# The outer dimension of a broadcast load and of a scattered store in a triangular inverse

## The chip, the cores and the metric

The kernel runs on one core of a Trainium2 chip. The metric is the device time of one execution in microseconds (us). Three runs of the kernel before took 3386.37, 3397.44 and 3398.57 us; their median is 3397.44 us.

## What is computed

A backbone of two layers works on 512 latent tokens and 256 context tokens of width 1024. Each layer has three parallel token mixers (a gated linear attention, a windowed attention, and RWKV-7 time mixing), whose outputs are gated, merged and projected, and then a SwiGLU feed-forward part. The change lies in the third mixer, which the reference runs forward and backward over the tokens, eight heads of 64, one token at a time:

```python
def step(S, inp):
    w_t, k_t, v_t, kk_t, a_t = inp[:5]
    sa = jnp.einsum('bhvk,bhk->bhv', S, kk_t)
    S = S * w_t[:, :, None, :] - sa[..., None] * (kk_t * a_t)[:, :, None, :] + v_t[..., None] * k_t[:, :, None, :]
    return S, jnp.einsum('bhvk,bhk->bhv', S, inp[5])
```

All operands are float32, and every matrix product of the layers is made of three with operands split in two parts (`wh`, `wl` of the weights, `hh`, `hl` of the activations).

## The kernel before

**The recurrence in chunks.** Class `Rwkv` takes the 768 tokens in 24 chunks of 32, four chunks to a group, six groups to each direction. The directions are two lanes, f and b, that `run` advances in turns (`lanes`, `ORDER`). For each group and lane three generators run: `prep` scales the loaded keys (`cp`, `kr`, `bk`, loaded by `load`) and makes the small products `X` on PE, masked by DVE (line 1507); `inverse` makes from `X` the inverse of one 32x32 unit triangular matrix per chunk and head; `chain` carries the state over the four chunks with `TT`, the inverses, as PE's weights (line 1595). `front` is `prep` followed by `inverse`; it runs one group ahead of `chain` in layer 0 and two groups in layer 1 (`ahead`). So there are 12 inverses in each layer, 24 in all.

**The inverse.** Two DMAs (line 1530) write the 32 triangular matrices of a group (4 chunks x 8 heads) from `X` to DRAM as `d1`, one after the other, 4 KB each. One DMA (line 1532) loads them into `L`, a tile of 128 partitions x 1024 floats: matrix m goes to partitions m, 32 + m, 64 + m and 96 + m, all four holding the same 4 KB. Partition 32 s + m then works on every fourth row of matrix m's inverse, the rows 4 a + s. `G` (128 x 8 x 32) starts as the rows of the identity: ACT issues a DMA from the constant `gid` (line 1537, called the reset here). In 31 steps of two instructions (line 1548, product into `ftmp`; line 1549, subtraction from `G`) the substitution is done, on DVE for lane f and on POOL for lane b. One DMA (line 1552) stores `G` to DRAM as `d2`, in runs of 32 floats, and one (line 1554) loads it in the layout that `chain` wants, as `TT`.

**What sets the order.** `L` and `G` have two buffers each, shared by both lanes. So an `L` is issued when the substitution two back has read its last, and a reset when the store two back has landed. Nearly all loads and stores are issued by SP, in one order, and each one can stand there for a semaphore; ACT issues the reset, `uv` and the store of the gates `gs` in its own stream of work. The completion of DMAs is counted on eight semaphores (DMAHW0 to DMAHW7 in the rows of order below), which are taken in turn: a DMA waits for the one that had its semaphore before. A planner (`TileContext` with its own model of times) decides the order of the instructions on each engine at build time, from the order of the generators and the dependences.

**What lies beside it.** In layer 0, `fill` gives PE projections (16 gate jobs and 8 branch jobs) between the lanes' turns. In layer 1 the same jobs are tied to the recurrence by `paced`: past a start of 150 products, 3.3 products are let go for every step noted by `hop`.

Of the kernel before, what the change touches and what calls it, by code (L numbers as in the profile page):

```python
# [1216 lines left out]
class Rwkv:  # L1217
# [304 lines left out]
    def inverse(self, d, g, later):  # L1522

        nc, T = self.nc, self.T
        d1 = self.D.tile([2, 16, 32, 32], F32, name="d1", tag="d1", bufs=3)
        d2 = self.D.tile([8, 4, 32, 32], F32, name="d2", tag="d2", bufs=3)
        X = self.hs[d, g]["X"]
        for q in range(2):
            r0 = 0 if q == 0 else 96
            nc.sync.dma_start(d1[q].rearrange("u j i -> j u i"), X[r0:r0 + 32].rearrange("j e w p i -> j (e w p) i")[:, :, 0:32])  # L1530
        L = T.tile([128, 32, 32], F32, name="L", tag="L", bufs=2)
        nc.sync.dma_start(L.rearrange("u j i -> u (j i)"), d1.rearrange("q u j i -> (q u) (j i)").unsqueeze(0).to_broadcast([4, 32, 1024]))
        yield
        if later is not None:
            self.load(d, later)
        G = T.tile([128, 8, 32], F32, name="G", tag="G", bufs=2)
        nc.scalar.dma_start(G, self.I["gid"])
        tmp = T.tile([128, 128], F32, name="ftmp", tag="ftmp", bufs=2)
        eng = nc.vector if d == "f" else nc.gpsimd
        for n in range(31):  # L1540
            if d == "f":
                j, rows, cols = n, slice(0, n // 4 + 1), slice(n + 1, 32)
            else:
                j = 31 - n
                rows, cols = slice(j // 4, 8), slice(0, j)
            a, m = rows.stop - rows.start, cols.stop - cols.start
            t = tmp[:, 0:a * m].rearrange("q (a b) -> q a b", b=m)
            eng.tensor_tensor(out=t, in0=G[:, rows, j:j + 1].to_broadcast([128, a, m]), in1=L[:, j:j + 1, cols].to_broadcast([128, a, m]), op=ALU.mult)  # L1548
            eng.tensor_tensor(out=G[:, rows, cols], in0=G[:, rows, cols], in1=t, op=ALU.subtract)  # L1549
            if n % 8 == 7:  # L1550
                yield
        nc.sync.dma_start(d2.rearrange("m p (a s) i -> s (m p) a i", s=4), G)
        TT = self.hs[d, g]["TT"] = T.tile([128, 8, 32], F32, name="TT", tag="TT", bufs=4 if self.zout else 6)
        nc.sync.dma_start(TT, d2.rearrange("m p r i -> (p r) m i"))
        yield
# [177 lines left out]
def _consts():  # L1733
    f = np.float32
    C = {}
    p = np.arange(128)
    C["ident"] = np.eye(128, dtype=f)
    o = np.zeros((128, 32), f)
    o[:, 0] = 1
    C["ones32"] = o  # L1740
    sn = np.zeros((128, 4, 128), f)
    for j in range(4):
        sn[32 * j, j, :] = 1
    C["selN"] = sn
    s = np.zeros((128, 4, 32), f)
    for j in range(4):
        s[:64, j, 2 * j] = 1
        s[64:, j, 2 * j + 1] = 1
    C["selH"] = s
    C["selkk"] = np.ascontiguousarray(np.tile(s.transpose(2, 1, 0), (4, 1, 1)))  # L1750
    j, i = (p % 32)[:, None], np.arange(32)[None, :]
    m = np.zeros((128, 2, 64), f)
    m[:, 0, :32], m[:, 0, 32:] = j < i, j <= i
    m[:, 1, :32], m[:, 1, 32:] = j > i, j >= i
    C["rmask"] = m
    g = np.zeros((128, 8, 32), f)
    for s_ in range(4):
        for a in range(8):
            g[32 * s_:32 * s_ + 32, a, 4 * a + s_] = 1
    C["gid"] = g  # L1760

    T = np.arange(512)
    inv = 10000.0 ** (-np.arange(16, dtype=np.float32) / np.float32(16))
    inv = inv.astype(np.float32)
    row, col = (T // 64).astype(f), (T % 64).astype(f)
    ang = np.stack([row[:, None] * inv, col[:, None] * inv], 1).astype(f)
    cs, sn_ = np.cos(ang).astype(f), np.sin(ang).astype(f)
    cos = np.zeros((128, 512), f)
    sin = np.zeros((128, 512), f)
    rot = np.zeros((128, 128), f)  # L1770
    for h in range(2):
        for a in range(2):
            for x in range(2):
                for q in range(16):
                    r = 64 * h + 32 * a + 16 * x + q
                    cos[r], sin[r] = cs[:, a, q], sn_[:, a, q]
                    if x == 0:
                        rot[r + 16, r] = -1.0
                    else:
                        rot[r - 16, r] = 1.0  # L1780
    C["cos"], C["sin"], C["rot"] = cos, sin, rot

    gm = np.zeros((5, 128, 32), np.int32)
    for n, mm in enumerate((16, 8, 4, 2, 1)):
        a, b = (p % 32)[:, None], np.arange(32)[None, :]
        gm[n] = (a // (2 * mm) == b // (2 * mm)) & (a // mm != b // mm)
    C["gmask"] = np.ascontiguousarray(gm.transpose(1, 0, 2))
    C["gdiag"] = (2.0 * ((p % 32)[:, None] == np.arange(32)[None, :])).astype(f)
    sm = np.ones((128, 768), f)
    sm[:, ::128] = 0  # L1790
    C["gscan"] = sm
    import ml_dtypes
    q_, k_ = np.arange(128)[:, None], np.arange(128)[None, :]
    w = np.zeros((128, 2, 128), f)
    w[:, 0] = np.where(k_ >= q_, 0.0, -1e30)
    w[:, 1] = np.where(k_ <= q_, 0.0, -1e30)
    C["wmask"] = w.astype(ml_dtypes.bfloat16)
    C["identb"] = np.eye(128, dtype=f).astype(ml_dtypes.bfloat16)
    return C


def _layout(x, c, ctx, c_ctx, w_ada, b_ada, g_mix, g_ffn, w_in, w_gk2, b_gk, g_gla, sink, mu_shift, w0, w_w2, a0, w_a2,
# [58 lines left out]
    D["w3"] = tile_k(w_ffn3, HID)  # L1861
    D["w2"] = con(w_ffn2.reshape(L, HID, 128, 8, 128).transpose(0, 3, 2, 1, 4)).reshape(L, 8, 128, HID * 128)
    D.update(_consts())
    return D

# [14 lines left out]
```

## Time and profile before

| | before |
|---|---|
| median of three runs | 3397.44 us |
| profiled execution, its own time | 3397.11 us |
| its span | 3394.7 us |
| granted TensorE clock, mean of the span | 0.911 |
| PE busy | 3014.1 us (89%) |
| DVE, ACT, POOL busy | 1725.6, 1126.2, 942.1 us |
| DMA moved | 398.31 MB, mean 117 GB/s |

The profile is one execution. A row of a timeline gives start, duration and, in brackets, how long the engine had been idle and what ended that; a letter q behind an engine's name (SPq, ACTq) means its queue, where a DMA's duration is that of its issue, not of the transfer. In the chain of waits a DMA's piece runs from its issue to its landing. The names d<-X, L<-d, d<-G, TT<-d and G<-gid are the five DMAs of the inverse. PE is TensorE, DVE VectorE, ACT ScalarE, POOL GpSimd, SP SyncE. The granted clock is a share of 2.4 GHz.

### The profile page before, as it was taken

What the parts mean: (1) busy time and instruction counts of PE and PEld (TensorE: products, weight loads), DVE (VectorE), ACT (ScalarE), POOL (GpSimd) and SP (SyncE); (2) the same over time, 40 slices, a digit from 0 to 9 for tenths busy, and PEclk for the clock granted to TensorE, in tenths of its full rate; (3) what the DMA queues carried; (4) which work ended last, traced back from release to release, by engine and by line L of the source; (5) the groups of instructions that cost most, each with busy time, mean ns of one, the idle gap of its engine ahead of it and who ended that gap; (6) DMA issues with size and microseconds to landing.
All of it is one profiled execution on the core that took longest, in us unless ns stands there. A gap on an engine that the chain in (4) does not pass through costs nothing. (4 is left out here: it accounts for less than half of the span.)

```text
span 3394.7 us, 62575 instructions
## 1 busy us (share of the span) xinstructions
PE 3014.1 (89%) x25760; PEld 2403.8 (71%) x25760; DVE 1725.6 (51%) x3336; ACT 1126.2 (33%) x2226; POOL 942.1 (28%) x1344
## 2 busy tenths in 40 slices
PE   6999999867888989999999899698757779799998
PEld 3777877655666778888888787576535456688887
DVE  3175557756546754222223455656556665643335
ACT  3255444422323333211112444543222233332223
POOL 2033122245346432100001212322256454221102
PEclk8999999877787999999999899899867789799999
DMA  7421222543335561443222323123533444613233
GB/s 286 152 73 61 96 101 96 174 118 104 103 110 145 179 203 57 154 155 139 62 69 89 95 75 97 57 77 132 177 99 111 126 122 142 190 58 100 93 100 118
DMA packets 269373, 398.31 MB, mean 117 GB/s; under 512 B 94624, under 2 KB 179360, under 8 KB 269088
## 3 DMA queue, kind: packets, MB, share of 16 engines
q1 hardware_dynamic: 241888, 360.76, 33.7%
q10 hardware_dynamic: 27200, 33.56, 3.0%
q8 instruction: 202, 3.31, 0.4%
q14 instruction: 83, 0.68, 0.1%
HBM read 320.33 MB, written 73.92 MB: 116 GB/s over the span
## 5 line engine op out<-in xcount | busy, mean ns | idle before, releaser
L50 PE MATMUL px<-hh,wh 128*128 128x512 f32 x1584 | 657.1, 415 | 21.8 <-ACT wh L71 15.3
L50 PE MATMUL px<-hh,wl 128*128 128x512 f32 x1584 | 649.2, 410 | 29.4 <-DVE wl L72 29.4
L50 PE MATMUL px<-hl,wh 128*128 128x512 f32 x1584 | 647.2, 409 | 10.4 <-POOL hl L302 7.9
L71 ACT ACTIVATE wh<-raw 128x1024 fp32r<-128x1024 f32 (+1 forms) x314 | 326.2, 1041 | 834.2 <-PE pz L50 411.9
L72 DVE TENSOR_TENSOR wl<-raw,wh 128x1024 fp32r<-128x1024 f32 (+1 forms) x314 | 398.3, 1269 | 369.6 <-ACT wh L71 336.5
L50 PEld LDWEIGHTS px<-hh,wh 128*128 128x128 f32 x1584 | 312.3, 197 | 115.6 <-issue 24.5
L50 PEld LDWEIGHTS px<-hh,wl 128*128 128x128 f32 x1584 | 311.5, 197 | 107.3 <-DVE wl L72 34.6
L50 PEld LDWEIGHTS px<-hl,wh 128*128 128x128 f32 x1584 | 312.3, 197 | 82.9 <-POOL hl L302 13.1
L673 POOL TENSOR_TENSOR al<-fs,ah 128x768 fp32r<-128x768 f32 (+1 forms) x44 | 85.0, 1931 | 728.1 <-ACT ah L672 728.1
L50 PE MATMUL pz<-hh,wh 128*128 128x256 f32 x872 | 254.5, 293 | 1.5 <-DVE fs L663 1.4
L50 PE MATMUL pz<-hl,wh 128*128 128x256 f32 x872 | 253.9, 291 | 2.2 <-DVE hl L304 1.7
L50 PE MATMUL pz<-hh,wl 128*128 128x256 f32 x872 | 253.2, 291 | 1.3 <-DVE wl L72 0.8
L50 PE MATMUL px<-y,wh 128*128 128x512 f32 (+1 forms) x512 | 152.6, 386 | 31.6 <-ACT y L123 14.1
L1548 POOL TENSOR_TENSOR ftmp<-G,L 128x60 f32<-128x60 f32 (+24 forms) x372 | 133.2, 358 | 165.8 <-DMA L<-d 78.7
L50 PEld LDWEIGHTS pz<-hh,wh 128*128 128x128 f32 x872 | 171.8, 198 | 10.1 <-issue 1.8
L50 PEld LDWEIGHTS pz<-hl,wh 128*128 128x128 f32 x872 | 172.5, 198 | 8.2 <-issue 2.2
L50 PEld LDWEIGHTS pz<-hh,wl 128*128 128x128 f32 x872 | 171.9, 197 | 6.4 <-issue 4.6
L1548 DVE TENSOR_TENSOR ftmp<-G,L 128x60 f32<-128x60 f32 (+24 forms) x372 | 106.1, 285 | 96.7 <-DMA L<-d 45.4
L1549 POOL TENSOR_TENSOR G<-G,ftmp 128x60 f32<-128x60 f32 (+24 forms) x372 | 137.0, 368 | 26.6
L50 PEld LDWEIGHTS px<-y,wh 128*128 128x128 f32 x512 | 95.4, 209 | 50.3 <-ACT y L123 14.9
L1603 ACT COPY uv<-up 32x128 f32<-32x128 f32 x384 | 98.2, 256 | 68.0 <-PE up L1595 50.7
L50 PE MATMUL px<-ah,wh 128*128 128x512 f32 x296 | 116.1, 393 | 0.0
(444 smaller groups left out, 5952.9 us busy)
## 6 DMA issues: line engine op xcount, KB each, us to landing
raw<-win SPq DMA_DIRECT2D x114, 512.0 KB
raw<-w SPq DMA_DIRECT2D x104, 512.0 KB
araw<-wada SPq DMA_DIRECT2D x96, 512.0 KB
raw<-w SPq DMA_DIRECT2D x48, 448.0 KB
kr<-krd SPq DMA_DIRECT2D x24, 512.0 KB
L<-d SPq DMA_DIRECT2D x24, 512.0 KB
gs<-gat ACTq DMA_DIRECT2D x24, 384.0 KB
raw<-wab SPq DMA_DIRECT2D x16, 512.0 KB
```

The costliest lines, as they stand in the source:

```text
L50: return self.nc.tensor.matmul(out, lhsT=lhsT, rhs=rhs, start=start, stop=stop)
L71: nc.scalar.activation(h[:, :n], raw[:, :n], AF.Copy)
L72: nc.vector.tensor_tensor(out=lo[:, :n], in0=raw[:, :n], in1=h[:, :n].bitcast(F32), op=ALU.subtract)
L673: nc.gpsimd.tensor_tensor(out=al, in0=s, in1=ah.bitcast(F32), op=ALU.subtract)
L1548: eng.tensor_tensor(out=t, in0=G[:, rows, j:j + 1].to_broadcast([128, a, m]), in1=L[:, j:j + 1, cols].to_broadcast([128, a, m]), op=ALU.mult)
L1549: eng.tensor_tensor(out=G[:, rows, cols], in0=G[:, rows, cols], in1=t, op=ALU.subtract)
L1603: nc.scalar.copy(uv[ru, p].rearrange("q e v -> q (e v)"), up[32 * p:32 * p + 32, :])
```

## The change

```diff
@@ inverse @@
         L = T.tile([128, 32, 32], F32, name="L", tag="L", bufs=2)
-        nc.sync.dma_start(L.rearrange("u j i -> u (j i)"), d1.rearrange("q u j i -> (q u) (j i)").unsqueeze(0).to_broadcast([4, 32, 1024]))
+        nc.sync.dma_start(L.rearrange("u j i -> u (j i)"), d1.rearrange("q u j i -> (q u) (j i)").unsqueeze(1).to_broadcast([32, 4, 1024]))
...
-        nc.sync.dma_start(d2.rearrange("m p (a s) i -> s (m p) a i", s=4), G)
+        for s in range(4):
+            nc.sync.dma_start(d2.rearrange("m p (a s) i -> s (m p) a i", s=4)[s], G[s::4])
@@ _consts @@
     for s_ in range(4):
         for a in range(8):
-            g[32 * s_:32 * s_ + 32, a, 4 * a + s_] = 1
+            g[s_::4, a, 4 * a + s_] = 1
```

Matrix m now goes to partitions 4 m to 4 m + 3, so that the load's source steps through 32 matrices outermost and repeats each four times, where it stepped through 4 copies of all 32. Partition 4 m + s works on the rows 4 a + s; the constant `gid` follows. The store is cut in four, one for each s, each from 32 partitions (every fourth) into 32 blocks of `d2`. The bytes are the same: 512 KB for a load of `L`, 128 KB for the four stores of one `G`. SP issues 72 DMAs more (4 for 1, 24 times). Lines behind 1552 move down by one.

The planner's order changes in the two recurrence stages. On SP, at the second round of layer 1, before (DVE_49 and Pool_49 are waits for lane f's and lane b's substitution):

```order
L1532 DMA L<-d_23411 128x1x1024 [waits DMAHW2_49,DVE_49]
L1552 DMA d_23134<-G 4x256x32 [waits DMAHW3_49,DVE_49]
L1532 DMA L<-d_23417 128x1x1024 [waits DMAHW6_49,DMAHW7_49,DMAHW4_49,Pool_49]
L1552 DMA d_23140<-G 4x256x32 [waits DMAHW5_49,Pool_49]
L1554 DMA TT<-d_23134 128x8x32 [waits DMAHW3_49]
```

and now:

```order
L1532 DMA L<-d_23453 128x1x1024 [waits DMAHW6_49,DVE_49]
L1553 DMA d_23170<-G 256x1x32 [waits DMAHW7_49,DVE_49]
L1553 DMA d_23170<-G 256x1x32 [waits DMAHW0_49]
L1553 DMA d_23170<-G 256x1x32 [waits DMAHW1_49]
L1553 DMA d_23170<-G 256x1x32 [waits DMAHW2_49]
L1553 DMA d_23176<-G 256x1x32 [waits DMAHW3_49,Pool_49]
L1553 DMA d_23176<-G 256x1x32 [waits DMAHW4_49]
L1555 DMA TT<-d_23170 128x8x32 [waits DMAHW6_49,DMAHW2_49,DMAHW7_49,DMAHW1_49,DMAHW0_49]
L1553 DMA d_23176<-G 256x1x32 x2
L1532 DMA L<-d_23459 128x1x1024
```

Lane b's load of `L` stood between the two stores; now it stands behind lane b's stores and behind lane f's `TT`, which waits for lane f's four stores.

On DVE, where the second substitution of lane f in layer 1 begins (X is the mask of lane b's products, on which PE's transposes and `d1` hang), before:

```order
L1480 SCALAR_TENSOR_TENSOR cs<-smask,cp 128x544
L1507 TENSOR_TENSOR X<-xp,rmask 128x512
L1488 COPY pc<-cp 128x16
L1507 TENSOR_TENSOR X<-xp,rmask 128x512
L1512 TENSOR_TENSOR bk<-bk,pc 128x1024
L1548 TENSOR_TENSOR ftmp<-G,L 128x31
L1549 TENSOR_TENSOR G<-G,ftmp 128x31
L1548 TENSOR_TENSOR ftmp<-G,L 128x30
```

and now:

```order
L1480 SCALAR_TENSOR_TENSOR cs<-smask,cp 128x544
L1548 TENSOR_TENSOR ftmp<-G,L 128x31
L1549 TENSOR_TENSOR G<-G,ftmp 128x31
L1548 TENSOR_TENSOR ftmp<-G,L 128x30
L1507 TENSOR_TENSOR X<-xp,rmask 128x512
L1549 TENSOR_TENSOR G<-G,ftmp 128x30
L1488 COPY pc<-cp 128x16
L1507 TENSOR_TENSOR X<-xp,rmask 128x512
L1512 TENSOR_TENSOR bk<-bk,pc 128x1024
```

The first product, which needs `L` and the reset of `G`, now stands ahead of both masks.

## Rows read from the trace of the kernel before

**Rows 1.** Stretches: recurrence of layer 0, what lies between, recurrence of layer 1.

```profile
core 0: us, PE busy (x) PEld busy (x) DVE busy (x) ACT busy (x) POOL busy (x), PEclk, DMA share, GB/s
680.00:1160.00 480.00, 394.26 (x5365) 299.60 (x5364) 272.93 (x663) 134.81 (x376) 228.57 (x487) 0.80 0.43 120
1160.00:2300.00 1140.00, 1081.61 (x7075) 898.44 (x7074) 496.33 (x825) 366.18 (x584) 202.83 (x150) 0.97 0.32 106
2440.00:2800.00 360.00, 243.88 (x3191) 173.22 (x3190) 207.98 (x527) 95.77 (x245) 186.00 (x421) 0.73 0.41 113
```

**Rows 2.** Lines, 2440 to 2800 us: count, busy us, mean ns, idle before, its releasers.

```profile
L1548 POOL TENSOR_TENSOR ftmp<-G,L 128x60 f32<-128x60 f32 (+24 forms) x177 | 62.5, 353 | 99.9 <-DMA L<-d 42.9 <-DMA G<-gid 38.8 <-issue 5.5
...
L1548 DVE TENSOR_TENSOR ftmp<-G,L 128x60 f32<-128x60 f32 (+24 forms) x186 | 54.5, 293 | 54.3 <-DMA G<-gid 25.3 <-DMA L<-d 23.7
```

**Rows 3.** Chain of waits, layer 1's recurrence: start us, us, what.

```profile
2444.13 9.64 DMA L<-d
...
2504.46 12.56 DMA d<-G
...
2557.74 12.65 DMA d<-G
...
2583.55 2.75 DMA G<-gid
...
2619.29 11.91 DMA d<-G
2631.28 9.26 DMA G<-gid
...
2649.57 3.71 DMA kr<-krd
...
2679.01 11.04 DMA d<-G
...
2728.85 5.73 DMA d<-G
...
2752.99 11.19 DMA L<-d
...
2766.89 2.10 DMA d<-X
2769.05 9.40 DMA L<-d
```

**Rows 4.** Timeline of SP, second round of layer 1: start us, us of issue, what.

```profile
2503.81 0.56 SPq L1532 DMA_DIRECT2D L<-d  x1
2504.46 0.56 SPq L1552 DMA_DIRECT2D d<-G  x1
2506.11 9.04 SPq L1532 DMA_DIRECT2D L<-d  x1
2515.25 0.53 SPq L1552 DMA_DIRECT2D d<-G  x1
2517.03 8.15 SPq L1554 DMA_DIRECT2D TT<-d  x1
```

**Rows 5.** Timelines of ACT, DVE and POOL, same round: reset and first products.

```profile
2517.04 0.39 ACTq L1537 DMA_DIRECT2D G<-gid  x1
...
2524.40 0.19 DVE L1548 TENSOR_TENSOR ftmp<-G,L 128x31 f32<-128x31 f32 x1 [4.32 <-DMA G<-gid]
...
2530.33 0.24 POOL L1548 TENSOR_TENSOR ftmp<-G,L 128x31 f32<-128x31 f32 x1 [22.83 <-DMA G<-gid]
```

**Rows 6.** Stretches: under one load of `L`; under a weight load.

```profile
1075.00:1079.00 4.00, 4.00 (x55) 3.21 (x54) 3.62 (x15) 2.46 (x6) 0.00 (x0) 1.00 0.25 78
3344.00:3346.00 2.00, 2.00 (x19) 2.00 (x19) 0.17 (x1) 0.92 (x2) 0.73 (x1) 1.00 0.92 362
```

**Rows 7.** PE's waits, layer 0's stage, then layer 1's: us, times, longest.

```profile
PE up L1595 <- DMA TT<-d: 17.2, 1, 17.2
...
PE up L1595 <- DMA TT<-d: 22.6, 1, 22.6
```

## Prediction

> **What bounds the kernel now.** I read the stretches first, then the chain of waits, then the queues in one round of it. The table by stretches tells where time can be won: between the two recurrence stages (1160 to 2300 us) PE is busy for 1081.61 of 1140 us, so nothing is to be had there, but in the recurrence of layer 0 it is idle for 480 - 394.26 = 85.7 us and in that of layer 1 for 360 - 243.88 = 116.1 us, at granted clocks of 0.80 and 0.73 [rows 1]. Only these two stages run `inverse`. In layer 1 the two engines that do the substitution, POOL for lane b and DVE for lane f, stood 99.9 and 54.3 us in front of its first product, nearly all of it for two DMAs: `L` and the reset of `G` [rows 2].
>
> The chain of waits (the profile follows it back through layer 1's recurrence, not to layer 0's) says that this idle time sets the end of the stage: in four rounds of lane f the store of `G` stands on it with 12.56, 12.65, 11.91 and 11.04 us, the broadcast load with 9.64 us at the start and 11.19 and 9.40 us at the end, and a reset with 9.26 us [rows 3]. A fifth store, which had no `L` just ahead of it, took 5.73 us, and loads of the same 512 KB with 128 partitions outermost take 3.71 us [rows 3]. So the store is slow because of what is ahead of it. SP's queue shows what: `L` at 2503.81, the store 0.65 us later, and then SP is held for 9.04 us by the issue of the next `L` and for 8.15 us by that of `TT` [rows 4]. ACT, which issues the reset only when the store has landed and releases a buffer of `G`, gets to it at 2517.04; DVE starts the next substitution at 2524.40, and POOL at 2530.33, having stood 22.83 us for the reset [rows 5]. And the width: while an `L` is alone in flight the mean busy share of the 16 DMA engines is 0.25, four engines' worth, while a weight load reaches 0.92 [rows 6].
>
> **The change, part by part.** *Removed:* the 24 loads of `L` with 4 outermost. *Put in their place:* 24 with 32 outermost, the same bytes. I have no row of such a load. Its price lies between 3.71 us (a load of the same size) and the 9.64 us of now; I take 4.3 us, near the low end, because `kr` is the nearest: the same bytes into the same 128 partitions, with 128 and not 4 outermost. By the Trainium skill (DMA: Bandwidth & Descriptors, section Why a DMA increments its semaphore by 16 and not by 1) a DMA uses the largest number of engines up to 16 that divides the slowest dimension of both sides, so 32 would give 16; the share of 0.25 agrees for an outermost 4, no run so far shows 32.
>
> *The store* was one DMA of 128 KB and becomes four of 32 KB. SP issues one in 0.56 us [rows 4], so four take 2.2 us. A store of 64 KB in runs of the same 128 bytes lands 2.10 us after its issue [rows 3]; that makes 4 x 0.56 + 2.1 = 4.3 us when nothing is ahead, and 5.0 us in the rounds where an `L` was issued just before, since that load now needs 4.3 us and all engines. The upper bound is four landings in series, 4 x 2.1 = 8.4 us; the lower is 4.3 us. The Trainium skill speaks against this cut (same page, section Rules for kernel authors): many small transfers should be one large one, as under 64 KB one pays mostly overhead. By that rule the term below would be the one of the second rival.
>
> The terms for layer 1, lane f, along the chain:
> - A, stores: 12.56 + 12.65 + 11.91 + 11.04 = 48.2 us become 4 x 5.0 = 20.0, and 5.73 becomes 4.3: 29.6 us less.
> - B, reset: the one of 9.26 us was in flight beside an `L`; another one took 2.75 us [rows 3]. 6.5 us less.
> - C, `L` at both ends, where no substitution covers it: 9.64 and 11.19 become 4.3 each: 12.2 us less. The last 9.40 us are lane b's and lie beside lane f's; they aren't counted. In the middle rounds `L` lies beside the store and reset and counts nothing.
> - D, SP: 12 x 3 more issues of 0.56 us are 20 us of its time in each layer. What lies on the path is in A; the rest is covered by the standing that goes (9.04 + 8.15 us in one round alone). If that standing stays, D costs up to 20 us per layer.
>
> A to C make 48.3 us. Lane b must gain as much, as the lanes share buffers of `L` and `G`; its 22.83 us [rows 5] say that it can. What is late next is the substitution itself and PE's recurrence; for these I take off a tenth: **44 us**.
>
> In layer 0 the chain isn't recorded. PE there waits 17.2 us once for `TT` behind the same queue of `L`, store, `L`, as it does for 22.6 us in layer 1 [rows 7]; the store's 7.6 us (12.6 - 5.0) come off it. Of the other 85.7 - 17.2 = 68.5 us of idle PE I take a fifth, 14 us; the bounds are 0 and the share that layer 1 gives back, 44 / 116 = 0.38, 33 us in all. So **21 us**.
>
> Order: the planner moves instructions only in the two stages. On SP all eight pieces come close together and lane b's `L` falls behind `TT`; DVE takes the first steps of the second substitution ahead of two masks. I price both at nothing: by A the reset and `L` are there about 10 us earlier than now, which covers the masks. If they aren't, see the last rival. The constant `gid` costs nothing.
>
> Sum: 44 + 21 = 65 us. The profiled execution took 3397.11 us (span 3394.7), 0.3 us under the median of the three runs, so it stands for them: 3397 - 65 = **3332 us**.
>
> **The rivals.**
> - *More comes free.* SP's stalls also hold weight loads and `bk`, `cp`, and ACT stands behind the reset; half of PE's idle time in both stages would be (85.7 + 116.1) / 2 = 101 us: 3296. For it: the issues of 8 to 9 us in rows 4, and the clock of 0.73, which could rise as PE idles less. Against it: planned orders have other waits. Chance 0.17.
> - *Four stores in series.* Each costs its landing: 8.4 us. A becomes 48.2 - 33.6 + 5.73 - 8.4 = 11.9, layer 0 the same share less; about 47 us in all: 3350. That is what the Trainium skill's rule on coalescing, named above, would make of it. Against it: the store of 64 KB is always one of two issued back to back, and the second still lands in 2.10 us. Chance 0.08.
> - *The recurrence takes over.* The rounds are then set by the steps of `chain` on PE, ACT and DVE; half of layer 1's sum is left, nothing in layer 0: 24 us, 3373. For it: two lanes share every engine, and in layer 0 PE is already busy for 82%. Chance 0.13.
> - *The load doesn't spread*, or reading each row four times slows it: `L` stays near 9.6 us, and the store's pieces on the same engines still stand behind it. No gain, and some of D: about 3400. Chance 0.07.
> - *Slower.* DVE stands at the first product of the substitution, and the masks of `X` are now behind it; on them hang PE's transposes, `d1` and the next `L`. DVE stood 54.3 us in six rounds [rows 2], 9 us each. If that stays (because `L` or the reset lands as late as now) and falls on the path, 54 us come against the 30 us of A: 24 us slower, 3421. It decides from 30 / 6 = 5 us of standing per round. Chance 0.05.
>
> **How the numbers follow.** The forecast has 0.5; its own range, from the bounds of store (4.3 to 8.4) and layer 0 (0 to 33), is 3310 to 3355. The range of 8 in 10 takes in the first three rivals and a little beyond: 3280 to 3382. A measurement of this kernel can tell about 0.5%, 17 us, from no change. Faster by more than that: 0.5 + 0.17 + 0.08 + 0.11 = 0.86; the third rival's upper end (0.02) and most of the fourth (0.06) are within 0.5%: 0.08; slower 0.06.
>
> **What would show it.** Right: in the chain of layer 1 no store over 6 us; `L` on it with 4 to 5 us; no issue on SP over 3 us; the idle time before `ftmp` under 30 us on DVE and under 50 us on POOL; a busy share well over 0.25 under an `L`; the stage of layer 1 some 45 us shorter and that of layer 0 some 20. Wrong: `L` still at 9 us; stores of 8 us or more; DVE standing 5 us or more per round in front of `ftmp` with `X` late; or all transfers short as said and the stages as long as before, with the time gone to PE's waits for `sblk`, `uv` and `ysb`.

## The result and the profile after

| | before | after |
|---|---|---|
| median of four runs | 3398.01 us | 3249.26 us |
| lowest and highest | 3386.37, 3403.33 us | 3244.56, 3251.97 us |
| profiled execution, its own time | 3397.11 us | 3250.64 us |
| span | 3394.7 us | 3248.8 us |
| granted clock, mean of the span | 0.911 | 0.936 |

The ratio is 0.9565, 95% interval 0.9538 to 0.9593: faster by 4.35%, 147 us at 3389 us, about the median of the kernel before over all comparisons (3382 to 3398 us), where 65 us were forecast. The time lies below the range (3280 to 3382 us). Below, a difference between kernels of separate comparisons is the difference of their ratios to before times 3389 us, each uncertain by some 10 us.

To compare the stages each is taken from the first issue of `L` to the first issue of a `wbc` weight load behind the recurrence. Before (columns as in [rows 1]; the clock stands behind the busy times):

```profile
675.00:1166.00 491.00, 405.26 (x5512) 308.44 (x5511) 277.87 (x668) 140.74 (x392) 230.97 (x488) 0.81 0.43 119
...
2444.00:2853.00 409.00, 291.96 (x3974) 203.80 (x3974) 227.18 (x555) 114.19 (x305) 210.14 (x464) 0.76 0.42 116
```

and after, with the stretch between the stages:

```profile
674.00:1083.00 409.00, 376.05 (x5507) 286.92 (x5508) 286.49 (x668) 140.99 (x393) 236.37 (x488) 0.92 0.48 143
1083.00:2364.00 1281.00, 1200.15 (x7790) 988.98 (x7791) 582.65 (x989) 415.72 (x696) 235.11 (x176) 0.95 0.34 113
2364.00:2708.00 344.00, 282.26 (x3970) 197.74 (x3968) 227.59 (x555) 113.73 (x305) 211.58 (x464) 0.81 0.48 138
```

Layer 0's stage lost 82 us, layer 1's 65, and nothing else moved. In layer 0 PE's idle time went from 491 - 405.26 = 85.7 to 33.0 us; the other 29 us are busy time: as many matmuls (5512, 5507) took 376 us instead of 405, at a granted clock of 0.92 instead of 0.81. In layer 1 idle time went from 117.0 to 61.7 us and busy time fell by 10 us, at 0.81 instead of 0.76.

Layer 1's chain of waits after, its rows for the five DMAs of the inverse from the stage's first `L` on (start us, us, what; the answer to [rows 3]):

```profile
2363.71 4.22 DMA L<-d
...
2411.11 2.18 DMA d<-G
2415.85 2.52 DMA TT<-d
...
2493.62 2.38 DMA d<-G
2496.17 2.63 DMA G<-gid
...
2559.97 1.95 DMA d<-G
2562.01 4.02 DMA G<-gid
...
2601.12 1.97 DMA d<-G
```

A store on it now is the last quarter, 1.95 to 2.38 us; one `L` is left. SP in the round that answers to [rows 4]:

```profile
2408.41 0.69 SPq L1532 DMA_DIRECT2D L<-d  x1
2409.18 6.49 SPq L1553 DMA_DIRECT2D d<-G  x6
2415.85 0.47 SPq L1555 DMA_DIRECT2D TT<-d  x1
2416.37 1.24 SPq L1553 DMA_DIRECT2D d<-G  x2
2417.65 0.62 SPq L1532 DMA_DIRECT2D L<-d  x1
2418.37 0.57 SPq L1456 DMA_DIRECT2D cp<-twdb  x1
```

The issues of 9.04 and 8.15 us are gone. The idle time before the first products, layer 1 from 2364 to 2708 us (answer to [rows 2]), and PE's waits for `TT` in both stages (to [rows 7]):

```profile
L1548 POOL TENSOR_TENSOR ftmp<-G,L 128x60 f32<-128x60 f32 (+24 forms) x186 | 67.0, 360 | 56.4 <-DMA L<-d 17.6 <-DMA G<-gid 14.2 <-DMA TT<-d 11.7
...
L1548 DVE TENSOR_TENSOR ftmp<-G,L 128x60 f32<-128x60 f32 (+24 forms) x186 | 53.6, 288 | 29.1 <-DMA L<-d 15.6 <-DMA G<-gid 8.2
```

```profile
PE up L1596 <- DMA TT<-d: 3.8, 2, 2.0
...
PE up L1596 <- DMA TT<-d: 8.4, 2, 8.0
```

Layer 0 shows what the prediction didn't look at. The waits for loads of `bk` and for `L` there (engine, line, releaser: us, times, longest), before:

```profile
DVE bk L1492 <- DMA bk<-bkdf: 36.5, 3, 24.2
POOL ftmp L1548 <- DMA L<-d: 35.8, 3, 18.1
...
DVE ftmp L1548 <- DMA L<-d: 21.7, 3, 11.6
DVE bk L1492 <- DMA bk<-bkdb: 13.9, 2, 8.8
```

and after:

```profile
DVE ftmp L1548 <- DMA L<-d: 9.3, 3, 3.9
...
DVE bk L1492 <- DMA bk<-bkdf: 4.1, 3, 1.9
```

DVE no longer waits for the other half of `bk` (POOL stood 14.3 us for it, once), and POOL's wait for `L` is down to 1.7 us.

### The profile page after: what moved, and what is told of

Its sections match the earlier page's. It is cut to its first block, busy times and chain, and to the rows that moved or that the text cites. A ratio compares the mean times of both kernels' runs of the same rounds, so it can differ in the third digit from the quotient of the medians.

```text
span 3248.8 us, 62663 instructions
## 1 busy us (share of the span) xinstructions
PE 2975.4 (92%) x25760; PEld 2376.0 (73%) x25760; DVE 1735.5 (53%) x3336; ACT 1126.6 (35%) x2226; POOL 951.7 (29%) x1344
## 5 line engine op out<-in xcount | busy, mean ns | idle before, releaser
L50 PE MATMUL px<-y,wh 128*128 128x512 f32 (+1 forms) x512 | 150.8, 383 | 25.7 <-ACT y L123 12.6
L1548 DVE TENSOR_TENSOR ftmp<-G,L 128x60 f32<-128x60 f32 (+24 forms) x372 | 114.0, 306 | 52.4 <-DMA L<-d 24.8
L1549 DVE TENSOR_TENSOR G<-G,ftmp 128x60 f32<-128x60 f32 (+24 forms) x372 | 114.2, 307 | 10.9
L231 POOL TENSOR_TENSOR sqa<-sqa,sq 128x256 f32<-128x256 f32 (+1 forms) x70 | 71.8, 1026 | 159.7 <-ACT sq L229 148.3
```

Source lines behind the costliest of these rows:

```text
L50: return self.nc.tensor.matmul(out, lhsT=lhsT, rhs=rhs, start=start, stop=stop)
L231: nc.gpsimd.tensor_tensor(out=acc[:, :n], in0=acc[:, :n], in1=sq[:, :n], op=ALU.add)
```

## The experiments

"Wide" is a load with 32 outermost, "narrow" one with 4. PE idle is the length of the stage less PE's busy time; the landing of `L` is the median over both stages from its issue to the last of its completions, worked out from the trace. The stages come from one profiled execution each; e3's took 15 us more than the median of e3's runs, so its stages are on the long side.

| kernel | ratio to before, 95% | layer 0, PE idle (us) | layer 1, PE idle (us) | `L` lands, us |
|---|---|---|---|---|
| before | 1 | 491, 85.7 | 409, 117.0 | 10.8 |
| e2 store in four | 0.9960 (0.9945 to 0.9975) | 491, 92.1 | 390, 88.7 | 10.6 |
| e3 load 8 outermost | 0.9763 (0.9735 to 0.9790) | 456, 58.1 | 373, 84.4 | 7.2 |
| e1 load wide | 0.9648 (0.9625 to 0.9671) | 429, 45.5 | 345, 64.0 | 4.5 |
| after (both) | 0.9565 (0.9538 to 0.9593) | 409, 33.0 | 344, 61.7 | 4.1 |
| e4 both, four `G` | 0.9566 (0.9544 to 0.9587) | 407, 30.1 | 337, 52.7 | 4.3 |

### The load alone and the store alone: e1, e2

e1 takes only the load's line of the change, e2 only the store's, in the old places:

```diff
-        nc.sync.dma_start(d2.rearrange("m p (a s) i -> s (m p) a i", s=4), G)
+        for s in range(4):
+            nc.sync.dma_start(d2.rearrange("m p (a s) i -> s (m p) a i", s=4)[s], G[32 * s:32 * s + 32])
```

> The load of L alone with 32 outermost, the store as before; every engine's order is that of before, row for row. (Matrix m lands in partitions 4 m to 4 m + 3 while gid and the store still count on the old places, so the values of the inverse differ; the time doesn't hang on them.) Theory: it is the load on four engines that holds SP, the store behind it and ACT behind the store; then this part alone gives most of the 149 us: 3270 to 3310 us, the load lands in 3.5 to 5.5 us, no issue of L or TT on SP over 3 us. Rival 1, the store is the slow part (128 KB in runs of 128 bytes from one DMA): at most 40 us come, 3360 or more, and the stores stay at 9 us or more. Rival 2, the planner's new order brings the gain: no more than the sum of my terms B and C, about 25 us.

> The store alone in four pieces (G's blocks of 32 partitions, old places), the load of L as before with 4 outermost; the planner's order moves. Theory: the four pieces still stand behind a load of 9 to 10 us on the same queue, so little comes: 3370 to 3410 us, and the last piece lands 9 us or more after its issue where an L is ahead. Rival 1, the store is the slow part: 3270 to 3310. Rival 2, the order brings it: 3300 to 3350, as the order here is close to that of the change.

e1: 3272.12 us, 0.9648, as the theory had it. e2: 3376.39 us, 0.9960, also as its theory had it. The stages of e1:

```profile
677.00:1106.00 429.00, 383.53 (x5503) 293.17 (x5504) 284.57 (x667) 140.64 (x392) 233.29 (x488) 0.88 0.46 136
...
2381.00:2726.00 345.00, 281.01 (x3975) 196.64 (x3975) 231.88 (x555) 114.55 (x305) 212.01 (x464) 0.82 0.48 138
```

The load alone gives 119 of the 147 us (0.0352 of 3389), with every engine's order as before: all that layer 1 wins (64 us) and three quarters of layer 0. One expectation missed: an issue of `TT` still took 3.98 us on SP. The store alone gives 14 us, all in layer 1; behind a wide load the store and the order that comes with it give 28, nearly all in layer 0. What of the 28 is the four pieces and what the order was not separated. In e1 the store is still one DMA, and it too became short. On layer 1's chain it now stands with

```profile
2426.50 6.80 DMA d<-G
...
2571.97 6.43 DMA d<-G
```

where it took 11.04 to 12.65 us behind the narrow `L`. With nothing ahead it takes 4.7 to 5.1 us in both kernels.

### A dose between: e3

```diff
-  d1.rearrange("q u j i -> (q u) (j i)").unsqueeze(0).to_broadcast([4, 32, 1024])
+  d1.rearrange("q u j i -> (q u) (j i)")[::2].unsqueeze(0).to_broadcast([8, 16, 1024])
```

> A dose between: the load of L with 8 outermost (16 rows of d1, every second, repeated eight times; 512 KB into the same partitions), store and every engine's order as before. (L then holds other matrices, so the values differ.) Theory: the share of the DMA engines under an L goes from 0.25 to about 0.5, the load lands in 5 to 6.5 us, and more than half of what the wide load alone gives comes: 3300 to 3345 us. Rival, it is not the width but the number of rows that are read or the repeated row: the load stays at 9 us and the time within 0.5% of before, 3380 to 3415.

3314.08 us, 0.9763: 80 us, two thirds of the wide load's 119. `L` lands in 7.2 us, later than expected. The busy share of the DMA engines under an `L` with 8 outermost, first with a store of `gs` in flight as well, then under `L` alone:

```profile
2416.50:2419.30 2.80, 0.00 (x0) 0.00 (x0) 0.00 (x0) 0.00 (x0) 0.00 (x0) 1.00 0.50 134
1041.50:1045.00 3.50, 3.50 (x49) 2.65 (x47) 3.19 (x13) 1.63 (x3) 0.00 (x0) 1.00 0.44 104
```

and in the changed kernel, under a wide `L` alone:

```profile
2544.60:2546.10 1.50, 1.50 (x39) 1.21 (x39) 0.00 (x0) 0.27 (x1) 1.34 (x5) 0.50 0.78 306
```

So 4, 8 and 32 outermost give 0.25 [rows 6], 0.44 to 0.50, and 0.78. The rule on 16 engines, which the prediction cites from the Trainium skill (DMA: Bandwidth & Descriptors, Why a DMA increments its semaphore by 16 and not by 1), agrees with the first two numbers; the third is above anything that 8 engines could give. The trace also notes 5, 9 and 16 updates of the semaphore for one such load. For the store it notes 5 for the single one, whose outermost dimension was 4, and 16 for each quarter: cutting the store changed its width as well as its number.

### Is it the hold on others? e5 to e8

A spare transfer of the same bytes and rows behind `L`, to a scratch that nobody reads; e5 narrow and e6 wide on SP, e7 narrow and e8 wide on ACT. Within a pair the order is the same on every engine.

```diff
+        d3 = self.D.tile([128, 1088], F32, name="d3", tag="d3", bufs=3)
+        nc.sync.dma_start(d3[:, 0:1024], d1.rearrange("q u j i -> (q u) (j i)").unsqueeze(0).to_broadcast([4, 32, 1024]))
```

> The changed kernel with a spare transfer that nobody waits for, issued by SP right behind each load of L: the 32 matrices once more, four times over, 512 KB from d1 to a scratch in DRAM, with 4 outermost. L itself stays wide and ahead of it. Beside the next run, which differs in the outer dimension alone and has the same order on every engine. Theory: the narrow transfer's price is what it does to all that stands behind it and beside it (bk, cp, stores, TT, weights at 8 to 13 us instead of 4 to 6), not the lateness of L; then this run is 60 to 130 us over the next one, more than half of it in layer 0. Rival: the lateness of L (and of its own store) is what counts; then the two runs lie within 25 us.

> The same spare transfer with 32 outermost. Theory: 512 KB over all engines, 3.5 to 6 us each and covered by what is idle (the DMA share in the stages is 0.48): 0 to 40 us over the changed kernel, 3250 to 3290. Rival: the bytes are the price, whatever their width; then this run is as slow as the one with 4 outermost, 3310 or more.

> The spare transfer with 4 outermost issued by ACT instead of SP, so that no DMA of SP's stands behind it on its own queue. Beside the next run, same order on every engine. Theory A, the four DMA engines are shared by both queues: SP's transfers that run beside it take 8 us or more as well, and the run is 50 us or more over the next one. Theory B, the hold is the queue's (later DMAs of the same queue wait behind the narrow one): SP's transfers land in 3.5 to 6 us, only uv, gs, the reset and yd, which ACT issues, are late, and the run is within 40 us of the next one.

> The spare transfer with 32 outermost issued by ACT. ACT must wait there for d1 to be written, so some time goes in this and in the run with 4 outermost alike: 3250 to 3310 us.

e5 3302.36 us (0.9733, 0.9709 to 0.9758), e6 3257.89 (0.9608, 0.9583 to 0.9633), e7 3302.39 (0.9736, 0.9716 to 0.9755), e8 3266.54 (0.9633, 0.9614 to 0.9651). The narrow spare costs 42 us more than the wide one on SP, between theory and rival, and 35 us on ACT, which is theory B's figure; 512 KB more, if wide, cost 15 us on SP. From the trace I worked out how long a transfer takes from issue to landing, in the two stages, apart for those issued while a narrow (or wide) one is in flight (count, median us):

```
                              SP, in flight   SP, else    ACT, in flight   ACT, else
before, L narrow               59  10.3       204  3.7      20  7.0         77  2.9
e3, L 8 outermost              57   7.4       204  3.7      16  5.5         81  3.0
e1, L wide                     41   5.2       222  3.8      11  4.2         86  3.0
e5, spare narrow on SP         74   8.1       283  3.6      18  5.2         79  3.3
e6, spare wide on SP           56   5.5       300  3.5      10  5.5         87  3.3
e7, spare narrow on ACT        85   7.0       274  3.5      13  6.0         84  3.6
e8, spare wide on ACT          38   5.1       318  3.5       5  4.6         92  3.6
```

In e7 the narrow transfer is on ACT's queue, and SP's still take twice as long beside it (7.0 for 3.5 us; 5.1 beside a wide one): the hold is not the queue's alone, if weaker across queues. In e5 ACT's few show none of it (5.2, and 5.5 beside a wide one). It isn't a matter of which transfers happen to be issued then: before, a store `d<-G` took 12.6 us beside an `L` and 4.9 else, a load `bk<-bkdf` 10.2 and 4.9 (medians). In all, the hold is worth some 40 us, not 119; 28 and 25 us of it are in layer 0's stage (440 us in e5, 412 in e6, 443 in e7, 418 in e8).

### Or the lateness of L? e9, e11, e15

e9 puts the two lines of e6's wide spare ahead of those of `L`:

```diff
+        nc.sync.dma_start(d3[:, 0:1024], d1.rearrange("q u j i -> (q u) (j i)").unsqueeze(1).to_broadcast([32, 4, 1024]))
         L = T.tile([128, 32, 32], F32, name="L", tag="L", bufs=2)
```

e11 loads `L` twice in a row and e15 three times, wide, each waiting for the one before:

```diff
+        for r in range(2):
+            nc.sync.dma_start(L.rearrange("u j i -> u (j i)"), d1.rearrange("q u j i -> (q u) (j i)").unsqueeze(1).to_broadcast([32, 4, 1024]))
```

> The spare wide transfer of e6 (512 KB, 32 outermost, SP) ahead of each L instead of behind it, so that L comes later by about one such transfer while what stands behind both finds the same load on the engines as in e6. Theory: the lateness of L itself is the other part of the gain (116.6 us of the wide load alone less the 44.5 us that the narrow spare cost over the wide one leave 72 us for some 6.3 us per load, 10.8 less 4.5); L lands 2 to 4 us later here, so 20 to 45 us over e6, 3275 to 3305 us. Rival: L's lateness is hidden as the substitution runs ahead of the chain; then within 12 us of e6, 3246 to 3270.

> The changed kernel with each wide load of L issued twice into the same tile; the second waits until the first has landed, and other transfers of SP stand between them. So L is complete about 4 to 5 us later, nearly as late as the narrow load (10.8 us), with the bytes of e6 and no narrow transfer anywhere. Theory: what the narrow spare didn't cost (116.6 less 44.5 us) is the price of L's lateness, 72 us for 6.3 us per load; with 4 to 5 us later this is 40 to 65 us over e6: 3295 to 3325 us, POOL and DVE standing before ftmp as long as before the change (over 100 us together). Rival: L's lateness is covered by the substitution two ahead, and the narrow load's whole price is its hold on others; then within 15 us of e6, 3245 to 3275.

> As e11 with three wide loads of L in a row, each waiting for the one before, so that L is complete some 13 to 15 us after the first issue, later than the narrow load of before (10.8 us), without any narrow transfer. Theory, lateness is cheap up to about 9 us and dear beyond: 60 us or more over e11, 3325 us or more. Rival, lateness costs evenly, 12 to 26 us for 4.5 us: 12 to 30 us over e11, 3280 to 3300 us.

e9: 3242.47 us (0.9584, 0.9554 to 0.9613). That is under both forecasts. Its dose wasn't delivered, `L` landed only 0.9 us later than in e6 (4.8, 3.9), so it says little; that a kernel with more to load has a shorter layer 1 (329 us against 340) shows how far a new order alone moves a stage. e11: 3267.77 us (0.9642, 0.9625 to 0.9659), `L` complete 9.5 us after its first issue, 12 us over e6: the rival. e15: 3257.04 us (0.9616, 0.9594 to 0.9637), `L` complete after 15.3 us, and no slower than e6, below either forecast. A late `L` costs 12 us at most here, where the order was planned with these loads in it.

### The narrow load at its own place: e12, e13, e14, e16, e17

e12 is e2, and each `L` waits until the store of the substitution two back has landed (`sync` adds a dependence on a semaphore, `rounds` keeps each round's instructions); e13 and e14 have the spare of e5 and e6 ahead of `L`, released like `L`:

```diff
+        if len(self.rounds) > 2:
+            for j in self.rounds[-3]["store"]:
+                self.K.sync(i, j)
```

```diff
+        if len(self.rounds) > 2:
+            self.K.sync(i, self.rounds[-3]["sub"])
```

e16 is e11 with the first of the two loads narrow, e17 with the second:

```diff
+        nc.sync.dma_start(L.rearrange("u j i -> u (j i)"), d1.rearrange("q u j i -> (q u) (j i)").unsqueeze(0).to_broadcast([4, 32, 1024]))
         nc.sync.dma_start(L.rearrange("u j i -> u (j i)"), d1.rearrange("q u j i -> (q u) (j i)").unsqueeze(1).to_broadcast([32, 4, 1024]))
```

> The kernel of e2 (narrow load of L, store in four pieces), where each L also waits until the store of the substitution two back has landed, so that the narrow load no longer stands ahead of the store and the reset; L itself comes some 4 to 6 us later than in e2. Theory, the price is the hold on the store and the reset directly behind L: the pieces land in 2 to 5 us instead of 8 to 11, and the run is faster than e2 in spite of the later L, 3330 to 3360 us (0.982 to 0.991 of before). Rival, what counts is when L is complete: slower than e2, 3385 to 3430 us.

> The changed kernel with the spare narrow transfer directly ahead of L and released with it (it waits for the substitution two back, as L does), beside the next run, which differs in its width alone and has the same order. Theory: here it holds what the old load held, L's completion and the store, and costs what the old one did: 80 to 130 us over the next run. Rival: no more than in e5, 35 to 55 us over the next run, and the missing 60 us of the decomposition come from the order of the instructions.

> The same with 32 outermost. 512 KB more ahead of L and of the store, over all engines: 10 to 40 us over the changed kernel, 3255 to 3290 us.

> As e11, but the first of the two loads of L with 4 outermost, the second with 32, which overwrites it: the narrow transfer stands at L's own place, ahead of the store, and L is complete some 15 us after its first issue; order as in e11 on every engine. Theory, hold and lateness cost more together than apart: 100 us or more over e11, 3368 us or more. Rival, they add up: 44 us of hold and 17 to 36 us for 6.3 us of lateness, 60 to 80 us over e11, 3328 to 3350 us.

> As e16 with the two loads of L swapped: first the wide one, then, when it has landed, the narrow one, with the order of e11 and e16 on every engine. (The second load puts the matrices into the old places, which gid and the store no longer count on, so the values of the inverse differ.) L is complete as late as in e16, 14 to 16 us after its first issue, but the store that follows L at once goes ahead of the narrow transfer. Theory, the hold on the store and the reset is the price: the store's pieces land in 2 to 5 us, and the run is 30 to 65 us over e11, 3295 to 3335 us (0.973 to 0.984 of before). Rival, it is the lateness of L beyond what the order was planned for, or the hold on whatever else is issued: 90 us or more over e11, 3355 us or more.

e12: 3384.64 us (1.0001, 0.9983 to 1.0018), slower than e2 as the rival had it, at the lower end of its times. Most pieces of its stores land in 2 to 4 us, and it is 14 us slower than e2. e13: 3329.07 us (0.9832, 0.9807 to 0.9857), e14: 3273.19 us (0.9666, 0.9639 to 0.9694): 56 us between them, nearer to the rival. In layer 1 the planner put most of the spare transfers behind `L` and the store after all, so there the pair says little more than e5 and e6. e16: 3374.62 us (0.9973, 0.9957 to 0.9988), e17: 3377.80 us (0.9972, 0.9958 to 0.9986): both 112 us over e11, with the order of e11, as the theory had it for e16 and the rival for e17. One narrow load in `L`'s own chain costs what the whole wide load gave. The stages of e11:

```profile
670.00:1102.00 432.00, 385.75 (x5509) 292.45 (x5510) 284.11 (x667) 141.20 (x392) 229.07 (x488) 0.87 0.50 150
...
2380.00:2726.00 346.00, 277.53 (x3971) 195.09 (x3969) 229.04 (x555) 113.79 (x303) 208.93 (x464) 0.83 0.53 156
```

and of e16:

```profile
676.00:1172.00 496.00, 402.55 (x5492) 303.26 (x5477) 276.71 (x667) 139.73 (x390) 227.50 (x488) 0.81 0.45 130
...
2450.00:2840.00 390.00, 298.33 (x3950) 208.08 (x3947) 225.38 (x555) 113.37 (x304) 206.52 (x464) 0.75 0.48 138
```

64 and 44 us longer, with the clocks of before. That e17 is as slow as e16 decides against my theory for it: there the store goes ahead of the narrow load. From e17's list of DMA issues (the last number is the median from issue to landing, us, of those whose landing the list can tell):

```profile
bk<-bkdf SPq DMA_DIRECT2D x12, 512.0 KB, 8.8
...
bk<-bkdb SPq DMA_DIRECT2D x12, 512.0 KB, 13.0
...
d<-G SPq DMA_DIRECT2D x96, 32.0 KB, 2.7
```

and from e11's:

```profile
bk<-bkdf SPq DMA_DIRECT2D x12, 512.0 KB, 5.5
...
bk<-bkdb SPq DMA_DIRECT2D x12, 512.0 KB, 5.5
...
d<-G SPq DMA_DIRECT2D x96, 32.0 KB, 3.1
```

Over all twelve of each, worked out from the trace, `bk` takes 9.2 and 11.2 us in e17, 5.5 and 5.5 in e11. The stores of e17 land even sooner than e11's, none later than 5.9 us. What is late is `bk`, and `L` itself, and no store stands on e17's chain in layer 1, but the second, narrow load does, three times:

```profile
2514.36 12.31 DMA L<-d
...
2665.84 9.92 DMA L<-d
...
2683.10 12.74 DMA L<-d
```

The idle time before the first products, whole program, of e15, whose `L` is complete 15.3 us after its first issue:

```profile
L1549 POOL TENSOR_TENSOR ftmp<-G,L 128x60 f32<-128x60 f32 (+24 forms) x372 | 130.6, 351 | 85.8 <-DMA L<-d 55.1 <-issue 4.8
...
L1549 DVE TENSOR_TENSOR ftmp<-G,L 128x60 f32<-128x60 f32 (+24 forms) x372 | 108.3, 291 | 51.3 <-DMA L<-d 40.8
```

and of e17, where it is complete after 16.3 us:

```profile
L1549 POOL TENSOR_TENSOR ftmp<-G,L 128x60 f32<-128x60 f32 (+24 forms) x372 | 127.5, 343 | 163.6 <-DMA L<-d 92.3 <-DMA raw<-win 31.3 <-issue 9.4
...
L1549 DVE TENSOR_TENSOR ftmp<-G,L 128x60 f32<-128x60 f32 (+24 forms) x372 | 103.9, 279 | 120.6 <-DMA L<-d 105.9 <-DMA G<-gid 4.0
```

`L` is about equally late in both, and POOL and DVE stand 137 us in the one and 284 us in the other. The planner gives a narrow and a wide load the same place (e1, e3 and the pairs have one order each), so it counts on `L` too early where a narrow one is loaded, and the engines stand in front of work that other work could have preceded. In e15 it saw three loads and put other work first: between the first issue of an `L` and the first product DVE is busy for 5.3 us and POOL for 3.6 in e15, for 3.4 and 1.8 in e17 (means of 12, from the traces). That this difference makes the standing is argued, not shown; `bk` and others are late in e17 too.

### More room behind the change: e4, e10

e4 gives `G` four buffers in layer 1, e10 also lets PE take more products per step (`PER`, which paces them, 3.8 for 3.3):

```diff
-        G = T.tile([128, 8, 32], F32, name="G", tag="G", bufs=2)
+        G = T.tile([128, 8, 32], F32, name="G", tag="G", bufs=2 if self.zout else 4)
```

```diff
-FREE, PER = 150, 3.3
+FREE, PER = 150, 3.8
```

> The changed kernel with four buffers of G in layer 1 instead of two, so that a reset there needs no store to have landed; the planner's order moves in layer 1's stage. Theory: of layer 1's 61.7 us of idle PE the part that hangs on ACT standing for the store (28.8 us of ACT's waits) goes: 15 to 30 us faster than the changed kernel, 3220 to 3235 us (ratio to before 0.948 to 0.952). Rival, the substitution and the recurrence set the rounds and the reset is covered: within 8 us of the changed kernel, 3241 to 3257.

> The changed kernel with four buffers of G in layer 1 (as e4) and PER 3.8 instead of 3.3: with the rounds of layer 1 shorter, PE may take more products of the projections per step of the recurrence. Theory: the 53 us of idle PE that e4 has left in layer 1 are in part steps in which no product was let go; 5 to 20 us under e4, 3225 to 3240. Rival: the idle pieces are waits of the recurrence and of weights (wl, X, sblk) that no pace fills: within 5 us of e4, 3240 to 3250, or slower, as the recurrence's own products come behind.

e4: 3244.53 us (0.9566), as the changed kernel: the rival, though layer 1's stage is 7 us shorter. ACT's 28.8 us of waiting for a store, which e4 no longer has, were covered. e10: 3257.31 us (0.9630, 0.9597 to 0.9662), 22 us over e4: PE took fewer products in the stage (3611 matmuls, 3980 in e4), and what follows it took 566 instead of 542 us. No run beats the changed kernel by more than can be told from no change.

## Why the prediction was right in direction and wrong in size

- **Width: right.** The share under an `L` is 0.78, `L` lands in 4.1 us (4.3 forecast), and three doses line up (e3, e1).
- **B, C and D: right as rows, but not all rows.** One `L` of 4.22 us stands on layer 1's chain, resets of 2.63 and 4.02 us. SP's 72 extra issues cost nothing: its issues took 118.5 us in layer 0 before and 99.8 after, 108.2 and 89.2 in layer 1, and none is over 2.5 us. But the chain before held three more long pieces, lane b's first `L`, a `TT` and a load of `bk`, which the sum left out:

```profile
2459.75 11.62 DMA L<-d
...
2517.03 11.34 DMA TT<-d
...
2695.62 12.39 DMA bk<-bkdb
```

At the medians of the changed kernel (4.1, 3.5 and 4.8 us) they would be 23 us shorter, by estimate.
- **A, the stores: right in the chain, wrong as a price.** A put 29.6 of layer 1's 48.3 us on the store. The stores did become short, and the reading that they were slow because of what was ahead of them holds. But e1 leaves the store whole, has it at 6.4 to 6.8 us on the chain, and wins as much in layer 1 (64 us) as the change does (65): there the cut added nothing. And where a load stays narrow, short stores don't bring the time: e17, with all of them short, is as slow as e16, and e12 no faster than before. The sentence that failed is "In the middle rounds `L` lies beside the store and reset and counts nothing": in e17 `L` stands on the chain in the middle rounds, in place of the store.
- **Layer 0: the term that failed by most.** "Of the other 85.7 - 17.2 = 68.5 us of idle PE I take a fifth, 14 us", with 33 us for the stage as the upper bound: a share without a reason. Idle time fell by 52.7 us, and 29 us more came from the clock: 82 us against 21. The waits for `bk` (50.4 us on DVE before, 4.1 after) and for `L` (57.5 us on DVE and POOL before, 11.0 after) show what was left out: I priced the five DMAs of the inverse, and none of the loads beside them, and `L` only on layer 1's chain. e5 to e8 price the hold on others by itself at 25 to 28 us in this stage; how the rest divides stays open.
- **The clock: not in the sum at all.** Layer 1 gave 65 us where 44 were forecast, 55 of them idle time and 10 the clock. So the 82 us that the forecast lacked are 32 of idle time in layer 0, 11 of idle time in layer 1, and 39 that the same products took less at a higher granted clock.
- **The range.** The forecast's own range, 3310 to 3355 us, doesn't follow from its two bounds: with the store at 8.4 us and nothing in layer 0 the sum is 28 us, 3369; with the store at 4.3 and 33 us in layer 0 it is 79 us, 3318.
- **The rivals.** "More comes free" named this, the stalls of weight loads and `bk` and a clock that rises as PE idles less, and gave 3296 us. Even that was too little: of 85.7 + 117.0 = 202.7 us of idle PE 108 went, about half as it said, and the clock gave 39 us more. Four stores in series fell: alone a quarter lands in 1.95 us, 0.6 us behind the one before, so a store takes 3 x 0.61 + 1.95 = 3.8 us where the single one took 4.7 to 5.1 with nothing ahead. The Trainium skill's rule on coalescing (DMA: Bandwidth & Descriptors, Rules for kernel authors) doesn't hold for this store, whose single form had 4 outermost; as the cut widened the store too, it is no test of the number of transfers alone. The slower rival fell: DVE stands 29.1 us before `ftmp` in layer 1, 54.3 before. POOL stands 56.4 us, a little over the 50 that I had named.

What is settled: the width of the one load makes 119 of 147 us, with the order unchanged. Its price arises in `L`'s own chain (e16, e17) and in what is issued beside it (e5 to e8); the store right behind it isn't needed for it (e17). What stays open: the hold alone is worth some 40 us, and the other 70 of e16's 112 us are put down, by difference, to an `L` later than the order counts on; a late `L` that the planner doesn't see, without a narrow transfer beside it, was not tried.

## What to carry to other kernels

The load with 4 outermost was slow for others too: price such a DMA by all that is issued while it is in flight, on every queue, and by the stages for which no chain is recorded, not by its own rows alone. Take all long rows of a chain, also those of the loads beside the change. A chain of waits says where time is spent, not what is won when one of its pieces goes; e1, with one half of the change, shows that the store stood on the chain because of the load. Where a planner orders the work and doesn't see a transfer's width, a load that is later than it counts on may cost far more than one that it knows to be late (some 70 us here against 12 at most, the 70 by difference and not shown alone).

## What was not expected of the hardware

- A narrow transfer delays others on both queues: beside it SP's took 10.3 us instead of 3.7, ACT's 7.0 instead of 2.9 (before); and a spare one on ACT's queue alone brought SP's to 7.0 us. One case went the other way: in e5 ACT's 18 transfers beside the narrow spare took no longer than beside a wide one (5.2 and 5.5 us).
- The clock was about a quarter of the gain, 39 of 147 us. With PE's idle time in layer 0 at 92 (e2), 86, 58, 46 and 33 us the granted clock of the stage was 0.82, 0.81, 0.84, 0.88 and 0.92, and the same products took 399, 405, 398, 384 and 376 us. The levels are 1.2 and 2.4 GHz; in the kernels with fewer gaps PE spent more of the stage at the upper one (e2, with the longest idle time, stands one hundredth above the kernel before).
